# Hybrid attention and SSD encoder step: projection steps spread over all attention rows, the SSD interleaved with the first half of the output projection

## The chip, the cores and the metric

The kernel runs on one core of one Trainium2 chip. The metric is the device time in microseconds of one execution. The engines are TensorE (PE: matmuls and transposes; PEld: its weight loads), VectorE (DVE), ScalarE (ACT), GpSimd (POOL) and SyncE (SP), which issues every DMA of this kernel. All data is 32-bit float; most matmuls split each operand into a high and a low part in fp32r and add three products.

## The reference, cut to what matters

One layer is run for a prompt of 1024 rows and for 128 sample rows (8 streams of 16), 1152 rows in all, in 9 blocks of 128 or 3 chunks of 384. Three mixers work on the same normalised input: SB (stick-breaking attention, 4 heads), SSD (Mamba-2, 8 heads) and FoX (attention with forget gates, 4 heads).

```python
proj = jnp.einsum('bnd,de->bne', u, p['w_in'])
sq, sk, sv, fq, fk, fv, fg, z, xbc, dt = split_last(proj, IN_SIZES)
logf = jax.nn.log_sigmoid((fg + p['fox_b_f']).astype(jnp.float32))
...
    w = jnp.where(valid, jnp.exp(jax.nn.log_sigmoid(z) + after), 0.0)      # SB: needs sq, sk, sv
...
    s = s + (fq[..., :, None] - fk[..., None, :])                          # FoX: cumulative sums of logf
    p = jax.nn.softmax(jnp.where(valid, s, -jnp.inf), axis=-1)
...
xbc_c = jax.nn.silu(causal_dwconv(xbc_pad, p['conv_w'], p['conv_b']))
dt = jax.nn.softplus((dt + p['dt_bias']).astype(jnp.float32))
y, h_final = ssd_scan(xs * dt[..., None], dt * A, Bm, Cm, h0, ssd_chunk)
ssd_o = rmsnorm(y * jax.nn.silu(z), p['ssd_norm_g'])
mix = jnp.concatenate([sb_o, fox_o, ssd_o], axis=-1)
out = jnp.einsum('bne,ed->bnd', mix, p['w_out'])
```

Behind it follow a cross-attention into 256 memory rows and a SwiGLU FFN, which the change does not touch.

## The kernel before, in words

The kernel is written in a tile framework. The Python code issues instructions in program order from generators that are advanced in turn; the framework then gives each engine a fixed order of its own, by program order as a priority and by what is ready in its own model of time. Tiles come from pools: a tile asked of a full pool waits until one of that pool is released. The pools that matter here are `act` (6 buffers of 128x3072: the normalised input `uc` takes all six until the input projection is done, then the SSD takes them), `st` (8), `ws` (7), `xc` (3), `so` (4, through `sg2_t`), `pt` (4), and the ring `wr`/`wh`/`wl` for weights and cached keys. PSUM has `pd` (2 banks), `pS` (2), `pT` (3) and `pO` (1).

First come the memory projection, the norms, and SB's Q, K and V projection. Then the attention stage. Its main loop is `pipeline(u0, LAG0, u1, LAG1)`: `u0` are the SB units, `u1` the FoX units, each 16 prompt units (4 heads by 4 pairs of row blocks: two `rows` steps and one `av` step, one yield each) and 4 sample units (one `rows` step, one `av` step) that read cached keys and values. A unit's `av` is issued 1 (SB) or 2 (FoX) units behind its `rows`. After each yield, a filler is advanced at a rate: `RATE[0]` steps a yield while the filler is the input projection, `RATE[1]` once it is the SSD.

The filler's projection part, `fill_s`, goes through FoX's Q and K (`dense_T`: 3 steps a job, 24 matmuls of 384 columns a step), FoX's V with the gates (`dense_N`: 9 steps of 24 matmuls of about 256 columns), then `fox_sums` (cumulative sums of the gates: a chain over DVE, PE, ACT and DMA with 4 yields), `pad_cols` (the convolution's past rows), and then the list `ORD`: `z0` and `z1` are halves of the gate z (9 steps each), `dt` is the softplus of the time steps, a pair `(j0, j1)` is the xbc jobs j0 to j1 - 1 (3 steps each, with a convolution on DVE behind the last), which take two `xc` tiles each. FoX heads take an `xc` tile for the row of gate sums (`fcb_of`), and FoX sample units one for theirs (`fkb`).

The SSD (`ssd_gen`) goes over 9 chunks of 128 rows, the samples first, in 51 steps: a chunk's steps are states, prepare, outputs, write and weights. Its results go to `mix_sc` in DRAM, rows 4 to 7; SB's and FoX's are rows 0 to 3.

`heads_out` loads rows 0 to 3 of `mix_sc` back, splits them (`load_rows`) and runs the first half of the output projection (`add_rows`: for each half j of the columns and each block, `half(blk, 0)` with k = 0, 1 and `half(blk, 2)` with k = 2, 3, 6 matmuls of 512 columns each, then an add into `h` on DVE): 36 steps. `ahead` is how many blocks the first halves run in front. `weave(fill, ho, WV, "ho")` advances WV steps of it for each remaining SSD step; 12 more follow, then the last chunk's write, the loads of the SSD rows, the rest, and `finish_rows` with the second half of w_out.

Of the kernel before, what the change touches and what calls it, by code (L numbers as in the profile page):

```python
# [17 lines left out]
P = 128  # L18
# [21 lines left out]
PD, PS_, PT_, PO_ = 2, 2, 3, 1  # L40
NACT = 3
FSC, CBE = "D", "DD"
WV = 2
GROUP = 4000
PIECE = 256
NL, NR = 3, 19
HN = 3
HP = {"av": 100, "xa": 100}
SPL = 2
ORD = ('z0', 'dt', (0, 8), 'z1')  # L50
XS, XH = 1, 2
X0, X1, XL = 2, 2, 2
REV = ()
RATE = (1.0, 1.1, 60)
C_SQ, C_SK, C_SV, C_FQ, C_FK, C_FV, C_Z, C_XBC, C_DT = 0, 256, 512, 768, 1024, 1280, 1540, 2052, 3076


# [5 lines left out]
def tile_hybrid_step(ctx: ExitStack, tc: tile.TileContext, a: dict):  # L63
# [22 lines left out]
    def act_t(dt=F32R, home=None):  # L86
        return (home or actp).tile([P, 3072], dt, tag="act", name="act")
# [4 lines left out]
    def st_t(dt=F32R):  # L92
        return stp.tile([P, 1024], dt, tag="st", name="st")
# [515 lines left out]
    def sg2_t(dt=F32):  # L609
        return ptp.tile([P, 256], dt, tag="so", name="so", bufs=4)  # L610
# [169 lines left out]
    def pad_cols():  # L780
        sct = xc_t()[0:24, :D]
        SP.dma_start(out=sct, in_=a["state_conv"][0].rearrange("b i c -> (b i) c"))
        tp = pd()
        for j in range(8):
            PE.transpose(tp[:, 24 * j:24 * j + 24], sct[:, j * P:(j + 1) * P], ident[:24, :24])
        DVE.tensor_copy(pads, tp[:, :192].rearrange("p (j b i) -> p j b i", j=8, i=3))
# [53 lines left out]
    def decode_units(m):  # L840
# [15 lines left out]
        def rows(p):  # L856
# [1 line left out]
                load_new()  # L858
            qsm = new[0]

            hold = act_t(F32) if m else None
            qt = (hold if m else st_t(F32))[:, 0:P]
            POOL.memset(qt, 0.0)
            q0 = qsm[:, 0:2, 0, 32 * p:32 * p + 32].rearrange("p n (b t) -> p n b t", b=2)
            qp = qt.rearrange("p (b n e t) -> p n e b t", b=2, n=2, e=2)
# [47 lines left out]
        def av(p, w, hold):  # L913
            vsm = new[1]

            wt = hold[:, P:P + 1024] if m else st_t(F32)
            wn = hold[:, P + 1024:2 * P + 1024] if m else sg2_t()[:, :P]
            for k0 in (0, 4, 8):
                nk = min(4, 9 - k0)
                tp = pT()  # L920
# [307 lines left out]
    drain(dense_T(w_in, uc, [(C_SK + P, consume_qk(3, 1, None, p_k[0], s_k[0]))]))  # L1228
    drain(proj_v(0, C_SV, p_v[0], s_v[0]))

    def fill_s():
        yield from dense_T(w_in, uc, [(C_FQ, consume_qk(4, 0, QS))])
        yield from dense_T(w_in, uc, [(C_FQ + P, consume_qk(5, 1, QS))])
        yield from dense_T(w_in, uc, [(C_FK, consume_qk(6, 0, None, p_k[1], s_k[1]))])
        yield from dense_T(w_in, uc, [(C_FK + P, consume_qk(7, 1, None, p_k[1], s_k[1]))])
        yield from proj_v(1, C_FV, p_v[1], s_v[1], extra=4)
        yield from fox_sums()
        pad_cols()
        for o in ORD:
            if o == "z1":  # L1240

                for hd in range(4):
                    tc.keep_in_program_order(
                        SP.dma_start(out=fs4.rearrange("(b h) i k -> b h i k", h=4)[:, hd],
                                     in_=fs_sc[hd].unsqueeze(1).to_broadcast([DEC_B, 4, PAST])))
                for p in range(4):
                    tc.keep_in_program_order(
                        SP.dma_start(out=fqs[:, p:p + 1], in_=fn_sc[8 * p:8 * p + 8, :]))
            if o[0] == "z":
                yield from z_proj(int(o[1]))  # L1250
            elif o == "dt":
                dt_softplus()
                yield
            else:
                yield from xbc_proj(*o)

    def mixed(m, at, fc, nxt):

# [40 lines left out]
            acc -= 1.0  # L1299


    def add_rows(w, k0, rows, h, ahead=0):


        for j in range(2):
            units = [w_unit([(w, j * 512, 512)], k0 + k, 2) for k in (0, 2)]
            sl = slice(j * 512, (j + 1) * 512)
            ps = {}

            def half(blk, k0):  # L1310
                if k0 == 0:
                    ps[blk] = (pd, pS)[blk % 2]()
                for k in (k0, k0 + 1):
                    hi, lo = rows(k, blk)
                    wh, wl = units[k // 2]
                    mm3(ps[blk], hi, lo, wh[:, k % 2, :], wl[:, k % 2, :], k == 0, k == 3)
                if k0:
                    DVE.tensor_tensor(out=h[blk][:, sl], in0=h[blk][:, sl], in1=ps.pop(blk), op=ALU.add)
            for blk in range(NBLK + ahead):
                if blk < NBLK:  # L1320
                    half(blk, 0)
                    yield
                if blk >= ahead:
                    half(blk - ahead, 2)
                    yield
# [32 lines left out]

    def load_rows(src, k):

        out = []
        for x in range(2):
            t = ws_t(F32R) if x < 1 or k < 3 else act_t()[:, :T]
            out.append(t)
        hi, lo = out
        for c0, c1 in ((0, T),) if k < SPL else ((0, SEQ), (SEQ, T)):
            SP.dma_start(out=f32(lo[:, c0:c1]), in_=src[k, :, c0:c1])
            ACT.copy(hi[:, c0:c1], f32(lo[:, c0:c1]))
            DVE.tensor_tensor(out=lo[:, c0:c1], in0=f32(lo[:, c0:c1]), in1=f32(hi[:, c0:c1]), op=ALU.subtract)
        return out  # L1370

    def chunk_t(home=None):

# [18 lines left out]
    def heads_out():  # L1392
        rows = [load_rows(mix_sc, k) for k in range(4)]
        more_h(NBLK)
        yield from add_rows(a["w_out"][0], 0, lambda k, b: [t[:, b * P:(b + 1) * P] for t in rows[k]], h, 3)

    ho = heads_out()
    weave(fill, ho, WV, "ho")
# [640 lines left out]
```

## Time and profile before

| | |
|---|---|
| median of 3 runs | 1907.74 us (1903.8 to 1910.01) |
| profiled execution: its time, its span | 1913.29 us, 1911.6 us |
| mean granted TensorE clock in it | 0.987 |
| busy share of PE, DVE, ACT, POOL | 96%, 46%, 43%, 33% |
| HBM read, written | 225.12 MB, 69.91 MB |

The profile's rows read: an engine's busy time in a stretch with the number of instructions in brackets; PEclk is the granted TensorE clock as a share of full speed; DMA share is the mean busy share of the 16 DMA engines. A row of a group of instructions has its line, engine, operation, tiles (out<-in), shape and count, then busy us, mean ns of one, and the idle time of the engine before them with what ended it. A row of the timeline has start, duration, engine, line, operation, tiles and count. Matmul durations overlap one another, so the price of one in a row of them is the distance between starts.

### The profile page before, as it was taken

The page shows a single profiled execution, that of the slowest core. Times are in us where ns is not written, and L with a number is a line of the kernel's source. Part 1 is how long each engine was busy: PE and PEld are TensorE (multiplying, and loading weights), DVE is VectorE, ACT ScalarE, POOL GpSimd, SP SyncE. Part 2 cuts the span into 40 slices and gives each one's busy share as a digit, 9 for nine tenths or more (in the row PEclk, how much of TensorE's full clock was granted, in tenths as well). Part 3 has the DMA queues.
Part 4 walks back from the last instruction along what each step waited for, and adds up shares of the span by engine and source line. Part 5 has one row for each costly group of instructions (what it writes and reads, how often), then busy time and mean ns, then how long its engine had stood idle before and what let it go on. Part 6 is the DMA issues. An engine that isn't in the chain of part 4 may idle for free.

```text
span 1911.6 us, 32359 instructions
## 1 busy us (share of the span) xinstructions
PE 1835.4 (96%) x12120; PEld 1640.8 (86%) x12120; DVE 887.5 (46%) x1794; ACT 823.0 (43%) x1759; POOL 622.5 (33%) x923
## 2 busy tenths in 40 slices
PE   7989998999988889999999999999999999999998
PEld 5889887888866777899998889999999999788886
DVE  3421323466546874354444387333333333455554
ACT  6532544446556762243433275333333333344443
POOL 7632235344224663211102105454444543000000
PEclk9999998999999999999999999999999999999999
DMA  9455645437679684344558124223332223556572
GB/s 334 144 158 161 196 140 148 148 90 207 185 204 282 224 281 135 111 144 152 187 197 280 67 83 119 70 70 81 87 76 70 69 70 104 194 193 231 181 243 90
DMA packets 291070, 296.64 MB, mean 155 GB/s; under 512 B 80093, under 2 KB 242885, under 8 KB 290913
## 3 DMA queue, kind: packets, MB, share of 16 engines
q1 hardware_dynamic: 290912, 294.57, 49.6%
q8 instruction: 95, 1.56, 0.3%
q14 instruction: 63, 0.51, 0.1%
HBM read 225.12 MB, written 69.91 MB: 154 GB/s over the span
## 4 chain that ended last, share of the span: by engine, by line
PE 80%; DMA 8%; DVE 3%; POOL 3%; ACT 2%; issue 2%; SPq 1%; POOLq 0%; DVEq 0%; ACTq 0%
PE psd L1861 11%; PE psd L328 10%; PE psd L329 10%; PE psd L330 9%; PE pst L1861 8%; PE pss L1861 4%; PE pss L328 3%; PE pss L329 3%; PE pss L330 3%; PE pso L1861 2%; PE pso L594 2%; DMA act<-acsc 2%; PE pst L328 1%; PE pst L329 1%; PE pst L330 1%
## 5 line engine op out<-in xcount | busy, mean ns | idle before, releaser
L132 POOL TENSOR_TENSOR wl<-wr,wh 128x256 fp32r<-128x256 f32 (+2 forms) x184 | 141.3, 802 | 232.3 <-ACT wh L292 192.0
L328 PE MATMUL psd<-act,wh 128*128 128x384 f32 x576 | 199.1, 346 | 4.5 <-DVE sg L455 2.7
L330 PE MATMUL psd<-act,wl 128*128 128x384 f32 x576 | 197.6, 343 | 0.7 <-POOL wl L132 0.7
L329 PE MATMUL psd<-act,wh 128*128 128x384 f32 x576 | 197.9, 344 | 0.0
L1861 PE MATMUL pst<-bT,tr 128*128 128x256 f32 (+1 forms) x1068 | 155.0, 293 | 0.0
L1861 PEld LDWEIGHTS pst<-bT,tr 128*128 128x128 f32 x1068 | 144.9, 188 | 0.1
L330 PE MATMUL psd<-wh,act 128*128 128x512 f32 (+3 forms) x424 | 136.8, 324 | 0.0
L328 PE MATMUL psd<-wh,act 128*128 128x256 f32 (+3 forms) x414 | 133.4, 326 | 2.9 <-ACT wh L292 1.3
L1861 PE MATMUL psd<-bT,tr 128*128 128x320 f32 (+1 forms) x912 | 133.2, 295 | 1.1 <-ACT tr L1701 0.5
L329 PE MATMUL psd<-wl,act 128*128 128x256 f32 (+3 forms) x414 | 133.6, 324 | 0.1
L1861 PEld LDWEIGHTS psd<-bT,tr 128*128 128x128 f32 x912 | 124.7, 188 | 2.1 <-ACT tr L1701 1.0
L328 PEld LDWEIGHTS psd<-act,wh 128*128 128x128 f32 x576 | 109.4, 190 | 7.4 <-DVE sg L455 3.1
L132 POOL TENSOR_TENSOR tr<-u,tr 128x256 fp32r<-128x256 f32 x110 | 82.6, 780 | 100.2 <-ACT tr L1701 82.4
L330 PEld LDWEIGHTS psd<-act,wl 128*128 128x128 f32 x576 | 109.2, 190 | 2.8 <-issue 1.5
L329 PEld LDWEIGHTS psd<-act,wh 128*128 128x128 f32 x576 | 109.4, 190 | 1.4 <-issue 1.1
L253 POOL TENSOR_SCALAR sm<-sm 128x1 f32<-128x1 f32 (+2 forms) x27 | 8.7, 321 | 295.7 <-ACT y L1944 208.8
L132 POOL TENSOR_TENSOR ws<-ws 128x256 f32<-128x256 f32 (+2 forms) x100 | 69.1, 719 | 108.9 <-DVE ws L521 103.1
L1836 DVE TENSOR_TENSOR tr<-tr,pst 128x256 f32<-128x256 f32 (+1 forms) x86 | 38.6, 449 | 138.5 <-ACT tr L1833 105.6
L132 POOL TENSOR_TENSOR tr<-raw,tr 128x256 fp32r<-128x256 f32 x94 | 69.3, 767 | 85.4 <-ACT tr L1701 77.3
L292 ACT CAST wh<-wr 128x512 fp32r<-128x512 f32 (+2 forms) x90 | 52.3, 620 | 95.3 <-PE psd L330 33.5
L328 PEld LDWEIGHTS psd<-wh,act 128*128 128x128 f32 x414 | 79.5, 192 | 11.7 <-issue 2.5
L1701 ACT CAST tr<-tr 128x384 fp32r<-128x384 f32 (+1 forms) x70 | 37.7, 538 | 118.7 <-DMA tr<-hidsc 115.6
(625 smaller groups left out, 4687.6 us busy)
## 6 DMA issues: line engine op xcount, KB each, us to landing
u<-w_down SPq DMA_DIRECT2D x40, 512.0 KB
raw<-w_down SPq DMA_DIRECT2D x26, 512.0 KB
st<-qksc SPq DMA_DIRECT2D x48, 256.0 KB
wr<-w_in SPq DMA_DIRECT2D x44, 256.0 KB
tr<-hidsc SPq DMA_DIRECT2D x57, 192.0 KB
hidsc<-tr SPq DMA_DIRECT2D x34, 288.0 KB
qksc<-sg SPq DMA_DIRECT2D x48, 192.0 KB
wr<-cache_sb_k SPq DMA_DIRECT2D x32, 256.0 KB
```

Of the source, the lines that this page charges most:

```text
L132: POOL.tensor_tensor(out=out[:, a0:a1], in0=in0[:, a0:a1], in1=in1[:, a0:a1], op=op)
L253: POOL.tensor_scalar(v, ss, inv, EPS, ALU.mult, ALU.add)
L292: ACT.copy(hi, raw)
L328: PE.matmul(out, ah, bh, start=start, stop=False)
L329: PE.matmul(out, ah, bl, start=False, stop=False)
L330: PE.matmul(out, al, bh, start=False, stop=stop)
L594: return PE.matmul(po[r:r + 64, q_], vt[:, 2 * (k0 + i) + j, :], pfs[i][:, sl], start=start and k0 == 0 and (j == 0 or qp > 0), stop=k0 + ...
L1701: ACT.copy(hi, src)
L1836: DVE.tensor_tensor(out=at(out, g), in0=at(x, g), in1=ps[g][:, :GW[g]], op=op)
L1861: PE.matmul(dst[g][:, :GW[g]], x[:, ka], y[:, k, :], start=start and k == 0 and m == 0, stop=stop and k == 3 and m == 2, skip_group_check= ...
```

## The change

1. `ORD` is now z0, xbc jobs 0 and 1, "fs" (the copies of the gate sums for the FoX sample units, before: ahead of z1), xbc jobs 2 to 7, z1. `fox_sums` and `pad_cols` no longer stand between V and z0: `beside` advances them one yield after each step of z0, and `dt_softplus` after the first steps of xbc.
2. `RATE` goes from 1.0 to 0.65 projection steps a yield; the SSD's 1.1 stays. `WV` goes from 2 to 1.
3. FoX sample units take their query and weight tiles from `st` and `so`, as SB's do, instead of holding an `act` tile.
4. `heads_out` uses the two `pS` banks alone (before: `pd` and `pS` in turn) and runs one block ahead instead of three. `load_rows` loads and splits each row in two parts (1024 and 128 columns); the low part of row 3 goes to an `xc` and a `pt` tile instead of an `act` tile.

```diff
-WV = 2
+WV = 1
-ORD = ('z0', 'dt', (0, 8), 'z1')
+ORD = ('z0', (0, 2), 'fs', (2, 8), 'z1')
-RATE = (1.0, 1.1, 60)
+RATE = (0.65, 1.1)
...
-            hold = act_t(F32) if m else None
-            qt = (hold if m else st_t(F32))[:, 0:P]
+            hold = None
+            qt = st_t(F32)[:, 0:P]
...
-            wt = hold[:, P:P + 1024] if m else st_t(F32)
-            wn = hold[:, P + 1024:2 * P + 1024] if m else sg2_t()[:, :P]
+            wt = st_t(F32)
+            wn = sg2_t()[:, :P]
...
+    def beside(main, aux):
+        for _ in main:
+            next(aux, None)
+            yield
+        drain(aux)
+    def sums():
+        yield
+        yield from fox_sums()
+        pad_cols()
+    def steps():
+        yield
+        dt_softplus()
     def fill_s():
...
-        yield from fox_sums()
-        pad_cols()
         for o in ORD:
-            if o == "z1":
+            if o == "fs":
...
-            if o[0] == "z":
-                yield from z_proj(int(o[1]))
-            elif o == "dt":
-                dt_softplus()
-                yield
+                continue
+            if o == "z0":
+                yield from beside(z_proj(0), sums())
+            elif o == "z1":
+                yield from z_proj(1)
             else:
-                yield from xbc_proj(*o)
+                yield from beside(xbc_proj(*o), steps() if o[0] == 0 else iter(()))
...
-    def add_rows(w, k0, rows, h, ahead=0):
+    def add_rows(w, k0, rows, h, ahead=0, homes=(pd, pS)):
...
-                    ps[blk] = (pd, pS)[blk % 2]()
+                    ps[blk] = homes[blk % 2]()
...
     def load_rows(src, k):
-        out = []
-        for x in range(2):
-            t = ws_t(F32R) if x < 1 or k < 3 else act_t()[:, :T]
-            out.append(t)
-        hi, lo = out
-        for c0, c1 in ((0, T),) if k < SPL else ((0, SEQ), (SEQ, T)):
...
+        hi = ws_t(F32R)
+        if k < 3:
+            lo = ws_t(F32R)
+            parts = [(0, SEQ, lo[:, :SEQ]), (SEQ, T, lo[:, SEQ:])]
+        else:
+            parts = [(0, SEQ, xc_t(F32R)[:, :SEQ]), (SEQ, T, pt_t()[:, :T - SEQ])]
+        for c0, c1, lo in parts:
...
-        yield from add_rows(a["w_out"][0], 0, lambda k, b: [t[:, b * P:(b + 1) * P] for t in rows[k]], h, 3)
+        yield from add_rows(a["w_out"][0], 0, lambda k, b: rows[k](b), h, 1, (pS, pS))
```

More of the change, by code (lines that the diff above doesn't have):

```diff
@@ L1359, in load_rows, with row @@
     def load_rows(src, k):
-        out = []
-        for x in range(2):
-            t = ws_t(F32R) if x < 1 or k < 3 else act_t()[:, :T]
-            out.append(t)
-        hi, lo = out
-        for c0, c1 in ((0, T),) if k < SPL else ((0, SEQ), (SEQ, T)):
[L1367 to L1370, printed above, removed]
+        hi = ws_t(F32R)
[5 more added lines that the diff above has]
+        for c0, c1, lo in parts:
+            SP.dma_start(out=f32(lo), in_=src[k, :, c0:c1])
+            ACT.copy(hi[:, c0:c1], f32(lo))
+            DVE.tensor_tensor(out=lo, in0=f32(lo), in1=f32(hi[:, c0:c1]), op=ALU.subtract)
+        def row(b):
+            c0, _, lo = parts[b // 8]
+            return hi[:, b * P:(b + 1) * P], lo[:, b * P - c0:(b + 1) * P - c0]
+        return row
     def chunk_t(home=None):
```

## The prediction

> **What bounds the kernel now.** I read the page first: its busy line, TensorE's row of 40 slices (47.8 us each), and of the costliest groups the split of the weights, which is needed below.
>
> ```profile
> span 1911.6 us, 32359 instructions
> PE 1835.4 (96%) x12120; PEld 1640.8 (86%) x12120; DVE 887.5 (46%) x1794; ACT 823.0 (43%) x1759; POOL 622.5 (33%) x923
> PE   7989998999988889999999999999999999999998
> ...
> L132 POOL TENSOR_TENSOR wl<-wr,wh 128x256 fp32r<-128x256 f32 (+2 forms) x184 | 141.3, 802 | 232.3 <-ACT wh L292 192.0 <-DMA wr<-w_in 35.4 <-DMA osc<-pt 4.7
> ```
>
> TensorE bounds the kernel. What a reordering can win is the time in which PE is idle or runs at a lower granted clock; the row of slices is thinnest at the start and in slices 12 to 15. The change touches the attention stage alone, so the second view is that of windows, cut where the work changes: SB attention from 170 us, the gate sums at 276 to 306, forgetting attention (FoX) from 463, SSD beside it from 547, attention over at 725, the last SSD rows written at 752.
>
> ```profile
> core 0: us, PE busy (x) PEld busy (x) DVE busy (x) ACT busy (x) POOL busy (x), PEclk, DMA share, GB/s
> 170.00:276.00 106.00, 104.64 (x776) 95.12 (x774) 28.23 (x43) 40.78 (x95) 30.34 (x55) 1.00 0.57 174
> 276.00:306.00 30.00, 23.09 (x139) 16.66 (x138) 14.55 (x42) 16.59 (x36) 20.11 (x30) 0.77 0.80 194
> 306.00:463.00 157.00, 152.00 (x1130) 135.55 (x1129) 81.52 (x122) 70.91 (x169) 68.63 (x99) 1.00 0.47 137
> 463.00:547.00 84.00, 82.57 (x666) 74.31 (x666) 48.55 (x124) 50.45 (x110) 20.52 (x39) 1.00 0.75 222
> 547.00:600.00 53.00, 44.65 (x315) 32.77 (x312) 28.64 (x95) 31.56 (x69) 16.56 (x26) 0.94 0.71 205
> 600.00:725.00 125.00, 111.84 (x949) 86.87 (x946) 94.27 (x256) 88.30 (x192) 79.25 (x126) 0.97 0.74 246
> 725.00:752.00 27.00, 23.77 (x99) 18.59 (x98) 11.03 (x16) 8.03 (x13) 5.77 (x9) 0.94 0.38 131
> ```
>
> I count as lost the idle time (first number less PE busy) plus busy time times (1 - PEclk). That gives 1.4, 12.2 (6.9 idle, 5.3 clock), 5.0, 1.4, 11.0, 16.5 and 4.7 us, together **52.2 us**. This is the ceiling of the gain. The 27.5 us of 547 to 725 are FoX and SSD with no projection left to fill PE; the 12.2 us are the hole of the gate sums. The rest of the stage loses little.
>
> **The counts.** The attention pipeline yields 3 times for each of 16 head units and twice for each of 4 sample units: 56 yields for SB, 56 for FoX. The projection has 12 steps of q and k, 9 of v, 9 of z0, 24 of xbc, 9 of z1: 63 with matmuls, and 5 more before (4 in fox_sums, 1 for dt). The SSD has 51, the first half of w_out 36. Before, at rate 1.0, the 68 steps end at yield 68; 44 yields at 1.1 then hold 48 SSD steps. After, 63 steps at 0.65 end at yield 97, 15 yields hold some 15 SSD steps, and the other 36 go one for one with the 36 of w_out. The trace agrees with the old count: a FoX row has one L548, and 9 of 36 rows lie before 547 us.
>
> ```profile
> 463.00:547.00 84.00, 4.97 (x9) 1.00 0.75 222
> ```
>
> Prices of the steps come from the starts of matmuls in the timeline: three of 384 columns take 0.53 us, three of 260 take 0.37 us, six of 512 take 1.38 us.
>
> ```profile
> 489.94 0.34 PE L328 MATMUL psd<-act,wh 128*128 128x384 f32 x1
> 490.47 0.34 PE L328 MATMUL psd<-act,wh 128*128 128x384 f32 x1
> 255.86 0.28 PE L330 MATMUL psd<-wh,act 128*128 128x260 f32 x1
> 256.23 0.28 PE L330 MATMUL psd<-wh,act 128*128 128x260 f32 x1
> 741.69 0.39 PE L328 MATMUL pss<-wh,ws 128*128 128x512 f32 x1
> 743.07 0.39 PE L328 MATMUL psd<-wh,ws 128*128 128x512 f32 x1
> ```
>
> So an xbc step (24 matmuls) is 4.2 us, a z step 3.0 us and a w_out step 1.38 us of PE. None is added or removed; only what stands beside it changes.
>
> **Part 1, gate sums beside z0.** The chain of fox_sums goes from the Abs at 276.2 us to the matmul on hsel at 296.3 us.
>
> ```profile
> 276.18 0.24 ACT L402 ACTIVATE sg<-lf 128x36 f32<-128x36 f32 x1
> 288.47 0.63 ACT L292 CAST wh<-wr 128x528 fp32r<-128x528 f32 x1 [2.13 <-DMA wr<-w_in]
> 296.33 0.50 PEld L725 LDWEIGHTS psd<-so,hsel 32*128 32x128 f32 x2 [0.65 <-DVE so L721]
> ```
>
> Its 20 us now lie beside nine z0 steps (27 us of PE). The middle row is z0's weights, split late at 288 us, because their loads stood behind the sums; they now stand ahead. Of 12.2 us I leave 1. Its DVE operations, its four POOL masks and its DMAs (2 results out, the past gates in, fc_sc, fs_sc, fn_sc, the conv state in) are the same and keep their place on their queues, ahead of xbc. The dt chain beside the first xbc steps is off the path on the same ground.
>
> **Part 2, thinner cover in SB.** SB keeps 36 projection steps instead of some 51. Outside the hole it lost 6.4 us (1.4 + 5.0) in some 51 yields, 0.125 each. Bounds: the same per yield (7.0 us), or the 0.625 of the bare stretch (27.5 in 44 yields, 35 us). PE still has about two steps per head unit, far nearer the first row, so 1.5 times it: **10.5 us**.
>
> **Part 3, projection under FoX.** 41 yields get 27 steps. The nearest row is 463 to 547, FoX with z1 and the end of xbc: 1.4 us in 12 yields, 0.12 each, **4.9 us**; upper bound again 0.625, 26 us. One resource becomes scarcer. The xc ring has 3 buffers; xbc takes two for a job, a FoX head's row of sums one, a sample unit one. Before, most xbc jobs ran under SB, which uses none. A job's DVE work holds them:
>
> ```profile
> L771 DVE SCALAR_TENSOR_TENSOR xc<-xc,cols 128x1024 f32<-128x1024 f32 x24 | 32.0, 1332 | 0.0
> ```
>
> A wait there delays a copy out of PSUM, not PE at once, since two banks let the next two steps go ahead. I take 2 us, bounds 0 and 8 (six jobs late by one L771). The xbc stores and weight loads of six jobs move on SP behind the FoX cache loads, where PE waited already (7.9 us in 4 waits, below); the fs4 and fqs copies move ahead of those loads. The FoX sample units take st and so tiles instead of act, as those of SB do; I cost it at nothing, because SB runs so at 0.125 per yield.
>
> **Part 4, the last 15 FoX yields with 15 SSD steps.** Nothing changes in kind: 15 x 0.625 = **9.4 us**.
>
> **Part 5, 36 SSD steps with w_out.** One SSD chunk has 5 steps. Its matmul groups and POOL work read:
>
> ```profile
> 608.28 1.95 PE L1154 MATMUL psd<-act 128*128 128x64 f32 x16
> 610.06 0.61 PE L1166 MATMUL psd<-ident,sg 128*128 128x128 f32 x4
> 611.00 0.71 PE L1069 MATMUL psd<-act 128*128 128x128 f32 x4
> 611.59 1.13 PE L1094 MATMUL psd<-act 128*128 128x256 f32 x4
> 613.62 1.03 PE L1100 MATMUL psd<-act 128*128 128x256 f32 x4
> 618.92 0.60 PE L1054 MATMUL psd<-ident,act 128*128 128x128 f32 x4
> 619.36 0.38 PE L1058 MATMUL psd<-ident,act 128*128 128x128 f32 x2
> L132 POOL TENSOR_TENSOR sg<-sg,act 128x256 f32<-128x256 f32 x30 | 23.1, 788 | 3.2 <-DVE sm L542 2.2 <-DVE sm L257 0.7 <-DVE sg L1156 0.2
> L1030 POOL TENSOR_TENSOR act<-act 128x256 f32<-128x256 f32 x28 | 19.9, 727 | 12.5 <-PE psd L1094 12.4
> L1030 POOL TENSOR_TENSOR act<-act,hb 128x256 f32<-128x256 f32 x14 | 10.4, 764 | 0.0
> L1030 POOL TENSOR_TENSOR act<-act,dts 128x256 f32<-128x256 f32 x14 | 9.7, 711 | 17.6 <-ACT act L1055 17.6
> L254 POOL TENSOR_TENSOR sm<-sm,mhalf 128x1 f32<-128x1 f32 x8 | 4.4, 555 | 0.4
> ```
>
> PE: 6.4 us a chunk, and five w_out steps 6.9 us: 13.3 us. POOL: 67.5 us in the 7 chunks of 600 to 705, 9.6 a chunk; the splits of w_out (16 pieces at 0.8 us, the group quoted from the page) add 1.8. So PE stays the longer one, but by 2 us only. Bounds: no loss, and the old rate per SSD step, 27.5 / 48 = 0.57, 20.6 us. The upper is the rate in company of FoX, whose cached keys PE waited for (the first row quoted under rival b) and whose loads delayed the broadcast of acsc (the second); both go with FoX, so I take the lower half: **8 us**. Three more waits end up here. The start waits for FoX's last rows to pass through mix_sc, as now (**4.7 us**, 725 to 752). Before, half of w_out covered the last chunk's outputs; now blocks 0 to 5 of the second half must. And its last two weight tiles wait for ws and xc tiles that free only at the end of the first half: two splits (a cast of 0.63 us like the one at 288 us, then 8 pieces of 0.8 us on POOL, 7.0 us) against 12 + 6 matmuls (18 x 0.23 = 4.1 us): **3 us**.
>
> **Sum.** 10.5 + 1 + 4.9 + 2 + 9.4 + 8 + 4.7 + 3 = 43.5 us lost instead of 52.2: 8.7 us gained. The profiled execution took 1913.3 us (span 1911.6); its forecast is 1904.6. It stands 0.3% above the median 1907.7, so the median's forecast is **1899 us**. This kernel's measurement tells about 0.3% (5.7 us) from no change.
>
> On the clock: 12.8 of the 52.2 us are granted clock, and they fall in the rows with idle PE. The Trainium skill (TensorE: Matmul & The Clock Gate, Part 1) halves the clock after about 3.4 us without activity, and in Part 4 says that transposes do not count as activity. The trace agrees with the second more than the first: 0.97 in 600 to 725, though all the idle PE time in it is 13.2 of 125 us. By that rule SSD transposes set among w_out matmuls would keep full clock.
>
> **Rivals.** (a) *The holes really fill*: SB loses 7 us, FoX 4.9, its end half of 9.4, the start 4.7, nothing else: 21 lost, 31 gained, 1877 us. For it: the order on the engines goes by readiness as well as by the program. SB's first scores stand behind all of the V projection there, and run 39 us ahead of its last copy out of PSUM:
>
> ```profile
> 126.97 0.48 PE L561 MATMUL pss<-st 128*128 128x128 f32 x2
> 165.66 0.37 ACT L487 COPY so<-psd 128x256 f32<-128x256 f32 x1 [0.31 <-ACT wh L292]
> ```
>
> So ready projection can fill SB and FoX wherever the program has it. Against: w_out cannot fill FoX's end, whose rows it needs.
>
> (b) *The loss only moves*: SB at twice its rate (14), w_out and SSD at 12 instead of 8: 51 lost, 1907 us, no change. For it: FoX's waits on DMA are its own.
>
> ```profile
> PE pst L888 <- DMA wr<-cache_fox_k: 7.9, 4, 3.3
> L1079 DVE TENSOR_SCALAR act<-act 128x128 f32<-128x128 f32 x35 | 12.3, 407 | 4.2 <-DMA act<-acsc 3.4 <-DMA mixsc<-so 0.8
> L1318 DVE TENSOR_TENSOR st<-st,psd x16: 677/686/690, 732.5 to 1066.4; 128x512 f32<-128x512 f32 x16
> ```
>
> (c) *The two-bank hand-over in w_out blocks PE* (slower). w_out now has the two pS banks alone and one block of lead, so block b + 1 starts only when the add of block b - 1 (L1318, 0.69 us) is through DVE. If DVE has an SSD chunk's five L1079 ahead of it (2.0 us), PE stands, and the SSD's matmuls behind it. There are 18 hand-overs; one SSD step (1.3 us) lies between. The gain is gone at (8.7 + 8) / 18 = 0.93 us each; above 1.25 us it is slower by over 0.3%; at 2 us, 36 us are lost there instead of 8, and the time is 1927 us. The Trainium skill (same page, Part 3, The mechanism) has matmuls start strictly in order, which is what makes one wait everybody's.
>
> **How the numbers follow.** Forecast 0.33 (1890 to 1902), (a) 0.25, (b) 0.20, (c) 0.22. Faster 0.58, same 0.20, slower 0.22. The range goes from (a) to about half of (c): 1877 to 1918; the forecast's own range is 1888 to 1905.
>
> **What would show it.** z0's matmuls run between the sums' (lines of fox_sums spread over z0) with the clock at 1.00; SB ends some 55 us earlier and FoX takes as much longer as its 27 steps need; the last FoX output is stored 60 us or more before the last SSD one; PE idle in the SSD and w_out stretch under 10%; L1154 groups 13 to 15 us apart there. Wrong would be: that distance at 16 us or more; waits of w_out on L1318 over 0.9 us each; SB idle doubled; waits on xc in the DMA queue.

## The result, and the profile after

The changed kernel takes **1939.17 us** (median of 4 runs, 1933.84 to 1940.42) against 1908.66 us before: ratio **1.0159, 95% interval 1.0132 to 1.0186**, 30 us slower. The forecast was 1899 us, in a range of 1877 to 1918. The profiled execution took 1940.4 us (span 1938.7).

The page of the kernel after, its span, its busy line and TensorE's row of slices (now 48.5 us each):

```profile
span 1938.7 us, 32392 instructions
PE 1848.5 (95%) x12120; PEld 1646.4 (85%) x12120; DVE 888.4 (46%) x1796; ACT 824.6 (43%) x1761; POOL 621.9 (32%) x923
PE   7989988999989989899999999999999999999998
```

The work is the same (12120 matmuls); PE is busy 13 us longer, at a lower clock, and idle 14 us longer. The view of windows of the kernel after, cut where its own work changes: SB from 170, z0 from 280, FoX from 409, the projection over at 619, attention over at 687, the last add of w_out's first half at 776, the last SSD rows written at 815 us.

```profile
core 0: us, PE busy (x) PEld busy (x) DVE busy (x) ACT busy (x) POOL busy (x), PEclk, DMA share, GB/s
170.00:320.00 150.00, 139.41 (x1056) 120.39 (x1055) 43.69 (x55) 67.39 (x154) 62.29 (x100) 0.98 0.58 175
320.00:360.00 40.00, 37.27 (x330) 30.86 (x329) 20.90 (x57) 19.41 (x47) 17.18 (x28) 0.96 0.49 143
360.00:409.00 49.00, 48.99 (x337) 41.95 (x337) 23.25 (x45) 26.09 (x62) 17.26 (x25) 1.00 0.65 179
409.00:619.00 210.00, 192.74 (x1453) 166.60 (x1454) 108.92 (x293) 115.34 (x246) 46.58 (x82) 0.97 0.58 175
619.00:687.00 68.00, 63.31 (x516) 47.04 (x513) 43.51 (x126) 45.90 (x100) 29.63 (x45) 0.97 0.73 239
687.00:776.00 89.00, 80.15 (x387) 65.50 (x386) 52.00 (x100) 28.99 (x67) 56.96 (x87) 0.90 0.44 148
776.00:815.00 39.00, 33.38 (x155) 26.99 (x154) 22.54 (x36) 9.49 (x18) 26.96 (x39) 0.87 0.44 135
815.00:861.00 46.00, 44.68 (x224) 37.28 (x222) 26.21 (x45) 21.78 (x41) 10.53 (x15) 1.00 0.43 149
```

Counted as in the prediction (idle time plus busy time times one less the clock), SB loses 17.6 us, FoX with the projection 23.0, FoX's end with the SSD 6.6, and the rows behind the attention 16.9, 9.9 and 1.3. That is 75.3 us where 52.2 were lost before and 43.5 were forecast. Set beside the kernel before, SB loses what it lost (17.6 against 18.6 us), and so does FoX with all that stands beside it (29.6 against 28.9); the 23 us more are lost behind the attention (28.1 against 4.7). The 31.8 us above the forecast are most of the 35.8 us by which the profiled execution missed its own forecast (1904.6).

Three events carry the rest of the reading: the projection's last store of z (L798), the copy ahead of each of the SSD's nine stores (L1167; its last start is called the SSD's end here), and the last add of w_out's first half. Their rows by line in the kernel before, with count, shortest, median and longest time in ns, and first and last start in us:

```profile
L798 SPq DMA_DIRECT2D zsc<-sg x18: 319/382/3074, 306.7 to 546.5; - x18
L1167 ACT COPY sg<-psd x9: 573/582/591, 611.0 to 751.4; 128x512 f32<-128x512 f32 x9
```

and the add, in the timeline of the kernel before:

```profile
774.17 0.69 DVE L1318 TENSOR_TENSOR xc<-xc,psd 128x512 f32<-128x512 f32 x1 [0.69 <-PE psd L330]
```

The same three of the kernel after, and the group of L1154, which has 16 matmuls in each chunk:

```profile
L798 SPq DMA_DIRECT2D zsc<-sg x18: 320/382/1353, 321.0 to 619.3; - x18
L1167 ACT COPY sg<-psd x9: 562/585/587, 683.2 to 814.5; 128x512 f32<-128x512 f32 x9
L1332 DVE TENSOR_TENSOR xc<-xc,pss x2: 686/688/689, 739.6 to 776.4; 128x512 f32<-128x512 f32 x2
L1154 PE MATMUL psd<-act x144: 217/275/476, 662.8 to 803.7; 128*128 128x64 f32 x144
```

Before, projection, SSD and w_out's first half ended at 547, 751 and 774 us: the SSD lay wholly beside other work. After, they end at 619, 815 and 776: the SSD outlives w_out's first half by 38 us. The nine L1154 groups stand 17.4 us apart on average (the last begins at 802.1 us in the timeline).

### The profile page after: what moved, and what is told of

Same layout as the page of the kernel before. It is cut to its first block, busy times and chain, and to the rows that moved or that the text cites. A ratio compares the mean times of both kernels' runs of the same rounds, so it can differ in the third digit from the quotient of the medians.

```text
span 1938.7 us, 32392 instructions
## 1 busy us (share of the span) xinstructions
PE 1848.5 (95%) x12120; PEld 1646.4 (85%) x12120; DVE 888.4 (46%) x1796; ACT 824.6 (43%) x1761; POOL 621.9 (32%) x923
## 3 DMA queue, kind: packets, MB, share of 16 engines
q1 hardware_dynamic: 291200, 294.57, 48.5%
## 4 chain that ended last, share of the span: by engine, by line
PE 80%; DMA 7%; DVE 4%; POOL 3%; ACT 2%; issue 2%; SPq 1%; POOLq 0%; DVEq 0%; ACTq 0%
PE psd L1880 11%; PE psd L328 9%; PE psd L329 9%; PE psd L330 9%; PE pst L1880 8%; PE pss L1880 4%; PE pss L328 3%; PE pss L329 3%; PE pss L330 3%; PE pso L594 2%; PE pso L1880 2%; POOL wl L132 2%; PE pst L579 2%; PE pst L328 1%; PE pst L329 1%
## 5 line engine op out<-in xcount | busy, mean ns | idle before, releaser
L328 PE MATMUL psd<-act,wh 128*128 128x384 f32 x576 | 199.5, 347 | 10.7 <-DVE sg L472 6.2
L328 PE MATMUL psd<-wh,act 128*128 128x256 f32 (+3 forms) x414 | 134.9, 329 | 5.3 <-DVE lf L491 1.9
L330 PE MATMUL psd<-wh,act 128*128 128x256 f32 (+3 forms) x414 | 132.5, 321 | 0.0
L328 PEld LDWEIGHTS psd<-act,wh 128*128 128x128 f32 x576 | 109.3, 190 | 14.8 <-DVE sg L472 7.3
L328 PEld LDWEIGHTS psd<-wh,act 128*128 128x128 f32 x414 | 79.9, 194 | 14.5 <-issue 2.4
L329 PEld LDWEIGHTS psd<-wl,act 128*128 128x128 f32 x414 | 79.7, 193 | 7.2 <-issue 1.5
```

What stands on the lines that cost most here:

```text
L328: PE.matmul(out, ah, bh, start=start, stop=False)
L329: PE.matmul(out, ah, bl, start=False, stop=False)
L330: PE.matmul(out, al, bh, start=False, stop=stop)
```

## The experiments

All ratios are to the kernel before, on the same chip. "Lost" is the prediction's measure, summed over fixed windows cut at 170, 320, 410, 480, 560, 620, 680, 730, 780, 830 and 880 us. Edits are against the changed kernel unless another is named.

### First: which part of the change costs

**The rate back at one step a yield**

```
-RATE = (0.65, 1.1)
+RATE = (1.0, 1.1)
```

> The changed kernel with its projection rate put back from 0.65 to 1.0; all else as changed. Theory A (the 30 us lie in separate places that the thin rate opens: FoX sample units beside z1's weights, and the SSD left over beside w_out): both places close, since the projection ends at yield 63 and the SSD within the attention; what stays is the start of w_out behind FoX with two banks and one block of lead. 1905 to 1915 us. Rival B (the two banks and one block of lead, not the rate, cost the time): 1928 to 1940 us, little changed.

1909.13 us, ratio 0.9996 (0.9982 to 1.001). The projection ends at 522.8, the SSD at 701.1, w_out's adds at 771 us. The 30 us are gone with this one number; everything else in the change (sums beside z0, SSD beside w_out, banks) is still in, and costs nothing in sum.

**Two more banks and a longer lead for w_out**

```
-add_rows(..., h, 1, (pS, pS))
+add_rows(..., h, 3)                # homes (pd, pS)
```

> The changed kernel with the first half of w_out on four PSUM banks (pd and pS in turn) and three blocks ahead again; all else as changed. Theory A: of the end of the attention (687 to 713 us, 7.5 us idle and 0.74 clock on 18.5 us busy, together 12.3 us) 6 to 10 us come back, because blocks with k = 0, 1 can run before FoX's rows are back: 1929 to 1933 us. Rival B: 15 to 25 us come back, 1914 to 1924 us. Rival C (the SSD needs the pd banks for itself; sharing them with w_out stalls the SSD): 1942 us or more.

1949.39 us, 1.0209 (1.0181 to 1.0237): worse by 10 us. The L1154 groups show a gap from 678 to 713 us where w_out begins, and the adds end at 789. The SSD uses pd as well, and that sharing it holds the SSD up is the likely reason; it is not shown, since this run changes the banks and the lead together.

**z1 ahead of the last xbc jobs**

```
-ORD = ('z0', (0, 2), 'fs', (2, 8), 'z1')
+ORD = ('z0', (0, 2), 'fs', 'z1', (2, 8))
```

> The changed kernel with z1 ahead of xbc jobs 2 to 7, so that the second and third FoX sample unit stand beside xbc jobs (which hold one pair of weight tiles) and not beside z1 (which holds two of three pairs). Theory A: the wait of 7.3 us on cached values at 572 us, the 3 us wait behind it and the half clock that follows (10 us long) go, 10 to 15 us: 1924 to 1929 us. Rival (a like wait appears beside whatever projection runs there): 1936 to 1942 us.

1938.98 us, 1.0153 (1.0134 to 1.0173). The sample units no longer stand beside z1's weights, and from 409 to 619 us 18.2 us are lost instead of 23.0. The time stays all the same: the projection's last store (now xbc's) is at 608 us, w_out's adds end at 759 and the SSD at 809.7, and 730 to 780 us now loses 15.9 us instead of 2.6.

**The gate sums beside z0, alone, in the kernel before**

```
(against the kernel before)
-ORD = ('z0', 'dt', (0, 8), 'z1')
+ORD = ('z0', (0, 2), 'fs', (2, 8), 'z1')     # with beside(z_proj(0), sums()) and the dt steps
...
-yield from fox_sums()                        # behind V
-pad_cols()
```

> The kernel before with part 1 alone: gate sums and the conv rows beside z0, dt beside xbc, the copies of the sums behind xbc job 1; rate 1.0 and all else as before. If the hole of the gate sums (12.2 us of idle and clock at 276 to 306) closes as forecast: 1896 to 1900 us. Rival (the hole is the sample unit's loads and z0's late weights, not the sums): 1904 to 1910 us.

1910.02 us, 1.0004 (0.9992 to 1.0017). Two rows of windows of this run; in the kernel before, PE is busy 139.81 us at a clock of 0.95 in the first and 74.06 at 0.96 in the second:

```profile
170.00:320.00 150.00, 145.36 (x1136) 129.13 (x1135) 48.72 (x99) 62.77 (x144) 51.10 (x94) 0.99 0.57 168
480.00:560.00 80.00, 72.22 (x575) 60.07 (x574) 39.68 (x120) 46.69 (x104) 21.82 (x37) 0.94 0.64 197
```

170 to 480 us loses 10.1 us instead of 20.3, and 480 to 880 us loses 44.6 instead of 34.5: about 54.7 in both kernels. The hole was closed, and as much is lost later, some 3 us more in each of 480 to 560, 560 to 620 and 680 to 730. The likely reason is that the projection, now done at 525 us, leaves FoX bare earlier; this is argued and not shown. The time is that of the rival, but its ground (that the sums are not what opens the hole) is refuted by the first row.

### Second: what in the late tail costs

**More SSD steps a yield beside FoX's end**

```
-RATE = (0.65, 1.1)
+RATE = (0.65, 2.4)
```

> The changed kernel with the SSD's rate in the attention raised from 1.1 to 2.4 steps a yield, so that 36 and not 15 of its 51 steps are issued before the attention ends; the projection's 0.65 stays. Theory S (the SSD is a chain of its own that takes some 180 to 220 us from its first matmul in any company: 217 before, 194 changed, 180 with rate 1.0; its start is set by the end of the projection): program order changes little, its last write stays at 800 to 815 us, total 1930 to 1940 us. Rival P (it is late because the program spreads it over w_out): the last write comes 20 us or more earlier and the total is 1912 to 1922 us.

1937.39 us, 1.0137 (1.0114 to 1.016). The SSD ends at 811.0 us (814.5 in the changed kernel), FoX at 726.8 (689.6). Where the program puts its steps hardly moves the SSD's end.

**The rate at 0.8**

```
-RATE = (0.65, 1.1)
+RATE = (0.8, 1.1)
```

> The changed kernel with the projection at 0.8 steps a yield (ends at yield 79, before 68 and changed 97). Theory S: the SSD starts some 25 us earlier than in the changed kernel and the total lies between 1909 (rate 1.0) and 1939 (rate 0.65), near 1920 us. Rival (thin cover in SB and FoX is the loss, with an optimum between the rates): below 1905 us. Rival (a step: the SSD either fits into the attention or not): 1932 us or more.

1910.53 us, 1.0004 (0.9992 to 1.0016). Projection 562.5, SSD 744.1, adds 770 us. S had named a time near 1920 us; neither that nor a rival's time came. The loss is not linear in the rate, from 1.0 to 0.8 nothing, from 0.8 to 0.65 some 29 us.

**w_out's splits on VectorE instead of GpSimd**

```
-units = [w_unit([(w, j * 512, 512)], k0 + k, 2) for k in (0, 2)]
+units = [w_unit([(w, j * 512, 512)], k0 + k, 2, eng=DVE) for k in (0, 2)]
...                                 # finish_rows: its four POOL become DVE as well
```

> The changed kernel with the splits of w_out (both halves) on DVE instead of POOL; all else as changed. POOL was busy 24 of 26 us at the start of the stretch of SSD and w_out (687 to 713 us), with 18.8 us of splits between 687 and 815. If they hold up the SSD (theory POOL): its chunks come 2 us closer, 10 to 18 us gained, 1921 to 1929 us. Theory S with a chain that waits mostly on itself: within 5 us of 1939. If DVE is the tighter engine there (52 of 89 us busy): 1942 us or more.

1943.59 us, 1.017 (1.0138 to 1.0202); the SSD ends at 825.0, ten us later. By its time this run is not told apart from the changed kernel. With the splits off GpSimd the SSD is no earlier, so they stand in its way there no more than they do on VectorE.

**The SSD held back until FoX is done**

```
-WV = 1
+WV = 0
-RATE = (0.65, 1.1)
+RATE = (1.0, 0.0)
```

> A measurement of the SSD by itself: projection at rate 1.0, no SSD step beside the attention, no w_out beside the SSD (rate 0, weave of 0), all else as changed; nothing is left out. It is slower on purpose. Theory S: with nothing beside it the SSD's chunks still come 11 to 14 us apart, and its length is 130 to 160 us. If it needs only its own POOL work (9.6 us a chunk) or less: 10 us apart or under, and then what stands beside it in the other kernels (w_out, FoX) is what stretches it.

A single run: 1938.96 us. The rows by line of this run:

```profile
L798 SPq DMA_DIRECT2D zsc<-sg x18: 319/400/766, 282.1 to 523.7; - x18
L1167 ACT COPY sg<-psd x9: 561/585/587, 704.1 to 810.3; 128x512 f32<-128x512 f32 x9
```

The projection is as early as at rate 1.0, and the time is that of the changed kernel, with the SSD's end where the changed kernel has it. From its first sample state (644 us) the SSD takes 166 us; with w_out's first half over at 726 us it has PE to itself until matmuls of the second half come at 789 us, and its L1154 groups still come 10 to 13 us apart (from 751 us on).

These four runs were set against **theory S**, to which the first four had led: the SSD is a serial chain over PE, ACT, DVE and GpSimd of some 180 us or more in company; its act tiles are the projection's until the projection ends; so the projection's end fixes the SSD's end, and what lies beyond w_out's first half is uncovered. The tiles are not shown to be what holds it: in the changed kernel its first loads into act tiles start at 568 us, while z1 still runs, and its first matmul at 620.5, behind the last step of z1 in the order of the program.

### Third: theory S in numbers

**The rate at 0.72**

```
-RATE = (0.65, 1.1)
+RATE = (0.72, 1.1)
```

> The projection's rate beside the attention rows is 0.72 in place of 0.65. Theory S (the SSD is a serial chain whose start is set by the projection's end, and it costs time only where it ends past the first half of the output projection at about 775 us): the projection ends near 589 us, the SSD's last write lands at 774 to 780 us, and the total is 1910 to 1917 us. Rival, the total follows the rate in a straight line between 0.65 (1939) and 0.8 (1910.5): about 1925 us.

1921.54 us, 1.0057 (1.0036 to 1.0078). Projection 593.8, SSD 782.2, adds 786 us. The SSD came within some 2 us of the range that S named; the total did not: it lies between the two theories.

**0.65 beside SB, 1.0 behind it**

```
-acc += RATE[1] if done[0] else RATE[0]
+acc += RATE[1] if done[0] else RATE[0] if k < 56 else 1.0
```

> The rate stays at 0.65 for the first 56 yields, all of the rows beside which SB stood before and more, and is 1.0 after them. Theory S: the thinner cover of SB stays as in the changed kernel, but the projection ends near 575 to 580 us, the SSD's last write lands at 760 to 768 us, and the total is 1905 to 1912 us. Rival, the thinner cover of SB is itself what costs the time: over 1920 us.

1918.75 us, 1.0044 (1.0029 to 1.006). Projection 571.0, some 4 us ahead of the range named, SSD 761.6, as named, adds 778, and the total is 7 us above what S allows. Of the changed kernel's 30 us, 22 are gone with the earlier SSD (1.0159 to 1.0044), and 8 stay though the SSD ends ahead of the adds.

**The rate at 0.9 with the two banks**

```
-RATE = (0.65, 1.1)
+RATE = (0.9, 1.1)
-add_rows(..., h, 1, (pS, pS))
+add_rows(..., h, 3)
```

> The rate is 0.9, and the first half of the output projection takes the two banks pd and pS and runs three tiles ahead, as in the run of the banks. Theory S: with the projection over near 545 us the SSD is done early, so that sharing pd with it costs nothing, and the start of the output projection is quicker: 1900 to 1907 us; if the start of the output projection isn't what sets the time, about 1909 us. Rival, the shared bank costs what it cost at 0.65 (10 us): 1915 us or more.

1920.39 us, 1.0036 (1.0016 to 1.0057), in the rival's range. With pd shared the L1154 groups again show a gap, from 707 to 746 us; the SSD takes 203 us from its first step (556.8 to 759.5) where it takes 183 at 0.8. A gap goes with the old banks and the longer lead here too. What they cost at this rate isn't measured, as no run has 0.9 with the banks of the change. SB also loses 17.8 us from 170 to 320 us; why stays open.

**The changed kernel without the skip term**

```
-heads_tt(xD, xn, ndsk)
-pool_tt(t1, t1, xD, ALU.add)
```

> The changed kernel at its rate of 0.65, without the SSD's skip term: the product of x with d_skip and its addition are left out, about 3 us of GpSimd a chunk and nothing of TensorE; the output lacks that term. Theory S, with the SSD's chain passing through GpSimd: the SSD is 15 to 25 us shorter and the total 1915 to 1928 us. Rival, the total is set by TensorE's work in this stretch: within 5 us of 1939 us.

1935.6 us, 1.0129 (1.011 to 1.0149). The busy line of its page and the row of L1167 (here L1165):

```profile
PE 1841.0 (95%) x12120; PEld 1639.5 (85%) x12120; DVE 891.9 (46%) x1796; ACT 824.3 (43%) x1761; POOL 595.9 (31%) x887
L1165 ACT COPY sg<-psd x9: 567/586/588, 677.8 to 802.9; 128x512 f32<-128x512 f32 x9
```

GpSimd has 26 us less to do, and the SSD is 6 us shorter (614.6 to 802.9 against 620.5 to 814.5), the total 4 to 6 us: the rival's range. These 26 us of GpSimd's work are for the most part not in the chain, and the SSD is not shorter by the 15 us or more that S asked for; what else of the chain runs over GpSimd this run doesn't tell.

### Fourth: the SSD's start and SB's cover, each by itself

**The rate at 0.8, and only the SSD's start late**

```
-RATE = (0.65, 1.1)
+RATE = (0.8, 1.1)
-acc += RATE[1] if done[0] else RATE[0]
+acc += (RATE[1] if k >= 102 else 0.0) if done[0] else RATE[0]
```

> The rate is 0.8, which cost nothing, but the SSD may not start before yield 102, so that it begins near 620 us, as in the changed kernel, though the projection is over near 562 us. Theory S (the SSD's start sets the time): its last write at 805 to 815 us and 1930 to 1940 us in all. Rival, the projection's rate is what costs and the SSD's start is not: 1910 us, or up to 1917 us with the attention rows between 562 and 620 us left without cover.

1933.73 us, 1.0117 (1.0098 to 1.0137), against 1.0004 at 0.8 without the hold. Two rows by line and one of windows of this run:

```profile
L798 SPq DMA_DIRECT2D zsc<-sg x18: 320/380/972, 314.3 to 564.5; - x18
L1167 ACT COPY sg<-psd x9: 566/585/588, 684.1 to 805.6; 128x512 f32<-128x512 f32 x9
730.00:780.00 50.00, 36.43 (x184) 30.57 (x183) 26.90 (x53) 17.47 (x38) 35.59 (x55) 0.83 0.41 122
```

The last row is the one to read: w_out's first half is over at 752 us, and little but SSD is left for PE behind it: 19.8 us lost in 50, where the rate of 0.8 without the hold loses 0.7. The SSD's late start costs 22 us by itself, with the projection, its rate and SB's cover untouched; the bare FoX rows behind 560 us add little (8.7 lost from 560 to 620, against 4.7).

**1.0 beside SB's first 40 yields, 0.535 behind them**

```
-acc += RATE[1] if done[0] else RATE[0]
+acc += RATE[1] if done[0] else 1.0 if k < 40 else 0.535
```

> The rate is 1.0 for the first 40 yields and 0.535 after them, so that the projection ends at about the same yield (83) as in the run with 0.65 for 56 yields and 1.0 after them (571 us), but SB has the thick cover. If the thin cover of SB is what was left of the loss there: about 8 us less than that run, 1905 to 1911 us, and 170:480 loses some 10 us in place of 21. If the projection's end alone sets the total: the same as that run, 1916 to 1921 us.

**1895.05 us, 0.9917 (0.99 to 0.9935)**: faster than both kernels, by 15 and 44 us, and 10 us below the lower of the two ranges named. Its rows by line (L958: FoX's last output is the last of the eight), and below them rows of its windows:

```profile
L798 SPq DMA_DIRECT2D zsc<-sg x18: 320/390/537, 282.4 to 569.3; - x18
L958 DVE COPY so<-pst x8: 207/224/225, 237.6 to 687.6; 128x64 f32<-128x64 f32 x8
L1167 ACT COPY sg<-psd x9: 567/586/590, 637.6 to 752.7; 128x512 f32<-128x512 f32 x9
L1332 DVE TENSOR_TENSOR xc<-xc,pss x2: 689/689/689, 722.8 to 756.9; 128x512 f32<-128x512 f32 x2
```

```profile
170.00:320.00 150.00, 144.75 (x1097) 128.55 (x1097) 49.05 (x97) 62.71 (x145) 51.63 (x95) 0.98 0.59 169
320.00:410.00 90.00, 89.59 (x665) 80.37 (x664) 46.80 (x79) 42.32 (x99) 42.00 (x57) 1.00 0.47 141
680.00:730.00 50.00, 47.30 (x320) 39.51 (x320) 32.82 (x59) 20.48 (x42) 39.09 (x54) 1.00 0.59 198
```

The same two views of the run with 0.65 first and 1.0 behind, whose projection ends at the same time (571.0):

```profile
L958 DVE COPY so<-pst x8: 213/224/226, 220.8 to 707.5; 128x64 f32<-128x64 f32 x8
L1332 DVE TENSOR_TENSOR xc<-xc,pss x2: 673/680/687, 749.3 to 778.3; 128x512 f32<-128x512 f32 x2
```

```profile
170.00:320.00 150.00, 139.05 (x1059) 119.95 (x1057) 43.58 (x59) 67.41 (x155) 60.74 (x99) 0.98 0.58 172
320.00:410.00 90.00, 87.21 (x667) 73.97 (x666) 44.38 (x99) 46.82 (x111) 35.97 (x55) 0.98 0.60 170
680.00:730.00 50.00, 40.35 (x279) 31.02 (x279) 37.18 (x67) 24.73 (x51) 37.17 (x53) 0.90 0.67 226
```

With the projection's end within 2 us, the order of the rates is worth some 23 us. From 170 to 480 us the lost time is 10.6 against 21.3 us: SB's cover does cost, and S, which had only the projection's end, falls as a full account. The other 10.8 us lie behind 480, and the row of 680 to 730 alone differs by 11.0: with FoX over at 687.6 instead of 707.5, w_out begins while four SSD chunks are left to stand beside it, and both end together (752.7 and 756.9).

**1.0 for 40 yields, 0.65 behind them**

```
-acc += RATE[1] if done[0] else RATE[0]
+acc += RATE[1] if done[0] else 1.0 if k < 40 else RATE[0]
```

> The rate is 1.0 for the first 40 yields and 0.65 after them; the projection ends near yield 75 (about 550 us), between the runs at 1.0 and 0.8. If the two gains add (the loss of 170:480 as at 1.0, some 10 us, the loss from 480 on as at 0.8, some 26 us): 1896 to 1902 us. If a hole closed in one stage opens in another, as with the gate sums: 1906 to 1911 us.

1905.83 us, 0.9983 (0.997 to 0.9997): the two gains don't add, and the time is just below the rival's range. SB loses 6.6 us from 170 to 480, the best of all; but the SSD ends at 726.9, 42 us ahead of w_out's adds (769), and the start of w_out stands bare: 10.7 us lost from 680 to 730, where the run before loses 2.7.

### The runs side by side

"Lead" is the last add of w_out's first half less the SSD's end. The runs that keep the rate of 0.65 with another edit, the one with the SSD held until FoX is done and the one at 0.9 are left out of the table and follow below it.

| kernel | lost 170 to 480 | SSD ends | adds end | lead | lost 480 to 880 | ratio |
|---|---|---|---|---|---|---|
| rate 1.0 | 9.7 | 701.1 | 771 | 70 | 42.0 | 0.9996 |
| 1.0, then 0.65 | 6.6 | 726.9 | 769 | 42 | 36.6 | 0.9983 |
| before, sums beside z0 | 10.1 | 745.4 | 774 | 29 | 44.6 | 1.0004 |
| before | 20.3 | 751.4 | 774 | 23 | 34.5 | 1 |
| rate 0.8 | 19.9 | 744.1 | 770 | 26 | 26.4 | 1.0004 |
| 0.65, then 1.0 | 21.3 | 761.6 | 778 | 17 | 34.2 | 1.0044 |
| 1.0, then 0.535 | 10.6 | 752.7 | 757 | 4 | 23.4 | 0.9917 |
| rate 0.72 | 26.8 | 782.2 | 786 | 4 | 32.3 | 1.0057 |
| 0.8, SSD held | 21.0 | 805.6 | 752 | -53 | 50.1 | 1.0117 |
| the change, 0.65 | 23.9 | 814.5 | 776 | -38 | 52.0 | 1.0159 |

The first loss is SB's: 7 to 11 us with the sums beside z0 and a step in each of the first 40 yields, 20 to 27 otherwise. Before, that is the hole of the sums. Below a rate of 1.0 thin cover is the likely reason, but the size doesn't follow the rate: 0.9 loses 26.7. Nor are these values exact: the change and its runs with more SSD steps, with the splits on VectorE and without the skip term are alike up to there and read 20.3 to 26.4.

The second loss is that of FoX and the tail: 50 us and more where the SSD outlives w_out's first half (50 to 61 in the six runs left out that keep 0.65 or hold the SSD back), 37 to 45 where it is over 29 us or more ahead, 23 to 35 where it ends up to 26 us ahead. Inside the last group the lead does not order the runs, and 0.9 with the shared banks (lead 22) stands outside it with 37.2. The two losses nearly add up to the time; the run that has a low value in both is the fast one. The totals aren't exact sums: single profiles lie up to some 5 us from their medians.

## Why the prediction was wrong, by its own steps

Of the 31.8 us above the forecast, part 3 has 16.1, part 5 12.4, parts 1 and 2 together 6.1, and part 4 came out 2.8 lower. Parts 3 and 5 are the steps that failed: by the first the FoX rows won nothing, by the second the rows behind the attention lost 23 us more than before where 11 more were forecast, and that made the kernel slower.

**Part 5** costed the 36 SSD steps at PE's work plus a small loss, 13.3 us a chunk, and let SSD and w_out end together because the program advances them one for one. By its own numbers both would have ended some 104 us behind the attention (7.2 chunks at 13.3 us, and 8 us lost); measured are 89 us for w_out's first half and 128 for the SSD. Its own sign of error (16 us or more between L1154 groups) came: the seven groups left when the attention ended begin between 693.3 and 802.1 us, 18.1 us apart on average. w_out's ready matmuls ran ahead and were done at 776 us; the SSD was not done before 815. The start, the body and the end were put at 4.7, 8 and 3 us, 15.7 in all; measured are 28.1. Cut finer, it reads:

```profile
687.00:713.00 26.00, 18.46 (x80) 13.83 (x79) 19.89 (x34) 9.53 (x23) 24.06 (x37) 0.74 0.81 284
713.00:742.00 29.00, 29.00 (x139) 24.38 (x138) 14.27 (x33) 9.12 (x20) 11.79 (x19) 0.94 0.23 73
742.00:776.00 34.00, 32.69 (x172) 27.29 (x171) 17.84 (x36) 10.34 (x24) 21.11 (x33) 1.00 0.33 110
```

The start alone loses 12.3 us where 4.7 were put, the two rows beside w_out some 3, and 776 to 815 us 9.9. The 38 us in which the SSD outlives w_out's first half are not all bare: from 787 us on, matmuls of w_out's second half on the first chunks stand between its steps, and the loss lies mostly ahead of 794 us (the last view of this document). The omission stands one step earlier: the prediction had the SSD begin at yield 97 and asked what stood beside it, never when it would end against w_out's end. The run at 0.8 with only the SSD's start held back gives a late start its price, 22 us.

**Part 3**, forecast 4.9 + 2 us, measured 23.0: over 41 yields 0.56 us each, near the upper bound of 0.625 that stands for bare rows, not the 0.12 taken from the row of 463 to 547. So FoX with some 27 projection steps beside it loses about as much as it lost without them. No wait of TensorE on an xc tile is among those of 409 to 619 us. The largest is one on FoX's cached V; its row in the view of waits, and from the timelines the two groups of matmuls that read the cached V of one sample unit, with the loads between them:

```profile
PE pso L933 <- DMA vr<-cache_fox_v: 7.3, 1, 7.3
568.25 1.06 PE L933 MATMUL pso<-vr,st 128*32 128x128 f32 x32
569.35 1.63 SPq L942 DMA_DIRECT2D vr<-cache_fox_v  x2
580.20 1.94 PE L933 MATMUL pso<-vr,st 128*32 128x128 f32 x32 [7.34 <-DMA vr<-cache_fox_v]
```

The loads of the second half are issued when the first half's matmuls are over (569.3 us), and TensorE can go on at 580.2. These loads take tiles of the ring of which z1's weights hold two pairs, so that one pair is left to both halves; that this is the reason is argued from the program, and the run with z1 ahead of the last xbc jobs agrees: the wait is gone from its list. The prediction priced the sample units' st and so tiles, at nothing, and did not ask for this ring beside z1. In that run a wait of 6.7 us stands there instead (L1054, the SSD's first rows, on the last xbc store), and the total stays. The wait of 7.3 us is less than half of the 16.1 us by which this part missed; where the rest comes from is not told apart.

**Part 2**, forecast 10.5 + 1 (with part 1), measured 17.6. The direction was right, the factor of 1.5 too small; the order of the rates moves the loss of SB's stage by some 10 us (21.3 against 10.6 in the two runs with equal ends). At 0.65 the largest wait of 170 to 320 us is that of the projection's own matmuls on VectorE (L328 on L472, 4.1 us in three), which is not among the waits at 1.0. SB did end some 55 us earlier, as forecast (FoX begins at 409 us instead of 463).

**Part 1** was right where it stood: in the kernel before, alone, it wins 10 us from 170 to 480. It did not carry to the total, as the same 10 us were lost later. Its gain can be kept: the fast run loses 10.6 us in that stage and 23.4 behind it, the least of all there.

**Part 4**, 9.4 forecast, 6.6 measured: right.

**The rivals.** (c), the slower one, named the wrong place: waits of w_out on the adds came to 0.6 us once. (a) fell: SB, FoX and the start of w_out each lost more than its terms. (b), that the loss only moves, is nearest in kind: it is what happens at 1.0 and with the sums alone. None of the three had the SSD's end as the thing that moves.

**The clock.** The prediction read a rule on transposes as a promise for the tail: SSD transposes among w_out matmuls would keep full clock. The windows of 687 to 776 and 776 to 815 ran at 0.90 and 0.87. The timeline of TensorE in the kernel after (start, time, then the work, and idle time before it) shows how:

```profile
777.57 1.10 PE L1100 MATMUL psd<-act 128*128 128x256 f32 x4
780.50 0.66 PE L1054 MATMUL psd<-ident,act 128*128 128x128 f32 x4 [1.83 <-DVE sg L1096]
782.12 0.69 PE L1058 MATMUL psd<-ident,act 128*128 128x128 f32 x2 [0.96 <-ACT act L1055]
783.80 3.68 PE L1154 MATMUL psd<-act 128*128 128x64 f32 x16 [0.99 <-ACT act L1059]
787.24 0.77 PE L328 MATMUL pss<-ws,act 128*128 128x512 f32 x1
```

L1154 takes 3.68 us where it took 1.95 before: the clock is half from 781.6 to 791.9 us (the first row of the last view). No idle time here is over 1.83 us; but between 778.67 and 783.80, 5.1 us, PE has transposes alone (L1054, L1058). With the first half of w_out over, no matmul was there to stand between them. The Trainium skill (TensorE: Matmul & The Clock Gate, Part 1) asks for an idle window of about 3.4 us, and in Part 4 says that transposes don't count as busy in the same way. The trace agrees with the two together only in part: the clock fell 2.9 us after the last other matmul. The half clock of the start, from 709.9 to 716.8 us, fits neither rule: the 3.4 us ahead of it hold no transposes, but some 1.8 us of matmuls of L1154 and w_out and one idle time of 1.60 us. What drops the clock there stays open.

**What stays open.** What the SSD's chain consists of, step by step: taking 26 us of GpSimd's work out of it shortens it by 6 us. How much of the 16.1 us by which part 3 missed comes from the sample unit's wait and what follows it, and how much from thin cover, isn't known either. How much of the 10.8 us behind 480 us that the order of the rates won comes from FoX's thinner cover and how much from the tail's balance is not told apart.

## What to carry to other kernels

Filler work has an end as well as a sum: before rationing it, work out when the last filler that starts late (here the SSD, which begins when the projection is done) will end, and against which cover. Put the thick ration where the rows are barest and the thin one behind it, so that the serial filler and the last work beside it end together. A hole that is closed in one stage is a gain only if the work pulled forward is not missed in a later one: compare the loss of all stages, not of the one that was mended.

## What the runs showed of the hardware

A busy PE can be at half clock. From 781.6 to 791.9 us of the kernel after, PE is busy 85% of the time at a granted clock of 0.50; over 776 to 794 us, the stretch that holds the five rows of the timeline above, it is 79% and 0.72:

```profile
781.60:791.90 10.30, 8.79 (x29) 7.42 (x30) 6.19 (x8) 3.44 (x6) 10.30 (x14) 0.50 0.47 154
776.00:794.00 18.00, 14.22 (x56) 11.41 (x55) 10.20 (x13) 4.93 (x9) 17.84 (x25) 0.72 0.48 146
```
